# A scheduler advance of 300 instructions for reads of the accumulator in a two-layer hybrid block

## The chip, the cores and the metric

The kernel runs on one core of a Trainium2 chip. The metric is the device time of one execution in microseconds (us), all of it fp32 work. Engines are named as in the profile: PE is TensorE, DVE is VectorE, ACT is ScalarE, POOL is GpSimd, SP is the engine that issues most transfers; PEld is PE's loading of the stationary operand.

## The reference, cut to what matters

Two layers over 640 tokens (128 context, 512 latent), each a token mixer and a feed-forward block, with 1024 channels:

```python
m = jax.nn.silu(cond) @ p['w_ada'] + p['b_ada']            # six modulation vectors
h = rms_norm(x, p['norm1']) * (1 + sc1) + sh1
q, k, v, og, gkf, gkb, sb, sc, sx, fx, mg = jnp.split(h @ p['w_in'], pts, axis=-1)
o = gla_bidir(q, k, v, la_f, la_b, s0_f, s0_b)             # 4 heads, chunks of 64, both directions
y_a = (norm(o) * silu(og)) @ p['w_a_out']
y_b = (sb * dwconv3(sc * sx, conv_w)) @ p['w_b_out']
y_c = real(fft2(fx)) @ p['w_c_out']
x = x + g1 * ((g[0] * y_a + g[1] * y_b + g[2] * y_c) @ p['w_o'])   # g: sigmoid of mg
h = rms_norm(x, p['norm2']) * (1 + sc2) + sh2
x = x + g2 * ((silu(gate) * up) @ w_down)                  # gate, up = split(h @ w_up)
```

The change lies in how `h @ w_in` (and, in a few places, `h @ w_up`) leaves the accumulator, and in the reads of the gated linear attention (GLA) heads that run between.

## The kernel before

**Products.** Tokens lie along the free axis (640, in halves of 320), channels on the partitions. Every product keeps fp32 accuracy by three matmuls: high part by high part, high by low, low by high. Weights are streamed by SP into buffers `raw` (six of 1024 columns); the high part `whi` is a cast on ACT (line 139), the low part `wlo` a subtraction on DVE (line 140), each into three buffers of 1024 columns. PE takes them in the order of the stream, and the split runs two chunks ahead. In mean a matmul of 128x128 by 128x320 follows the one before it by the distance that the rows below show.

**Pairs.** Most of `w_in` and `w_up` goes through `pair` (line 249): two column blocks together, with seven half-size products of 12 matmuls where eight would be plain. The accumulator space (PSUM) is handed out as four tiles of two banks. A pair N of the mixer has the tile `w1p_Nb` for its bank y and `w1p_Na` for its banks x and b. In program order a pair does: product into x; ACT copies x to `s1` (line 276); product T1 into b; ACT copies b to `s5` (line 280); product T2 into y; DVE adds y to `s1` (line 283); ACT writes `s1` back into y (line 284); DVE adds `s1` to b (line 285); then 24 matmuls into x and b (B21 and B22), after which `done` copies the first result block out (for instance line 966); then product T3 into y; DVE adds `s5` to y for half of the second block (line 296); and, put off into the next pair by `last`, product T4 into y and the copy of y (line 300). So the 24 matmuls into `w1p_Na` wait for line 285, and T3 into `w1p_Nb` waits for line 284. Weight sums that the pair needs (`sb`, `sc`, lines 160 to 167) are made on DVE. There are 24 pairs in each mixer and 19 in each feed-forward block.

**Between products.** `tick_bg` steps generators that put other work between the products: a GLA head (`gla_head`: gate products `lg` at line 639, read by ACT at lines 641 and 642; two scans on DVE at lines 646 and 647; state steps on DVE at line 696, 14 in a head; attention products `af` and `ab` at line 703, read by DVE at lines 704 and 705; output products read by ACT at lines 719 and 720), and pieces of the modulation of the next layer (`ada`: products at line 371, ACT copy at line 377, transposes at line 380, DVE reduction at line 383). They take their PSUM tiles from the same four.

**What sets the order.** The order of instructions on each engine is made ahead of time by a list scheduler: among the instructions whose inputs its model takes for ready, the one with the lowest priority number goes first, and that number is the place in the program as written. Each engine then runs its list strictly in that order. Nothing in the code sets another priority.

Of the kernel before, what the change touches and what calls it, by code (L numbers as in the profile page):

```python
# [14 lines left out]
AF = mybir.ActivationFunctionType  # L15
ALU = mybir.AluOpType
# [7 lines left out]
T = 640  # L24
TH = 320
# [66 lines left out]
class Builder:  # L92
    def __init__(self, stack, tc, a):
        self.tc = tc
        self.nc = tc.nc
        self.a = a
        self.cp = stack.enter_context(tc.tile_pool(name="cp", bufs=1))
        self.wp = stack.enter_context(tc.tile_pool(name="wp", bufs=1))
        self.up = stack.enter_context(tc.tile_pool(name="up", bufs=N_UNITS))
        self.pp = stack.enter_context(tc.tile_pool(name="pp", bufs=4, space=PSUM))  # L100
        self.dp = stack.enter_context(tc.tile_pool(name="dp", bufs=1, space=DRAM))
        self.n = 0
        self.gens, self.later, self.ada_last, self.last_act, self.pending = [], [], None, None, None
# [144 lines left out]
    def pair(self, key, h, T12, T34, done):  # L248

        nc = self.nc

        def prod(o, w, c0, ops, first):
            for kb in range(4):
                sl = slice(c0 + kb * P, c0 + kb * P + P)
                lh, ll = w[0][:, sl], w[1][:, sl]  # L260
# [12 lines left out]
        x, b = p1[:, 0:TH], p1[:, 512:512 + TH]
        prod(x, wa, 0, B11, True)
        s1 = self.wp.tile([P, TH], F32, tag="s1", name=self.name("s1"), bufs=1)
        nc.scalar.copy(s1, x)
# [12 lines left out]
        prod(x, wa, 512, B21, False)  # L289
        del wa  # L290
        w = self.take(key, "c")
        prod(b, w, 0, B22, False)
        done(0, pv(p1))
        prod(y, w, 512, T3, False)
        z = self.wp.tile([P, T], F32, tag="z", name=self.name("z"), bufs=3)
        nc.vector.tensor_add(z[:, TH:T], y, s5)

        def last():
            prod(y, d, 0, T4, False)
            nc.scalar.copy(z[:, 0:TH], y)  # L300
# [72 lines left out]
    def ada_end(self, l, v, n, ps):  # L373
        nc = self.nc
        p = self.par[l]
        u = self.unit(cols=256, s="adas")
        nc.scalar.copy(u, ps[:, 0:256])
# [5 lines left out]
        nc.vector.tensor_reduce(mv, pm.rearrange("p (k j i) -> p k i j", k=2, i=32)[:, :, 0:2, :], op=ALU.add, axis=mybir.AxisListType.X)  # L383
# [250 lines left out]
    def gla_head(self, l, hd, gk, qd, kd, v, yos):  # L634
        nc = self.nc
        p = self.par[l]
        ps = self.psum("lg")
        for h in range(2):
            nc.tensor.matmul(ps[:, h * 512:h * 512 + TH], p["w_gk"][:, hd, :], gk[:, h * TH:h * TH + TH], start=True, stop=True)
        u1, u2, bc = self.unit(s="u1"), self.unit(s="u2"), self.unit(s="bc")  # L640
        nc.scalar.activation(halves(u1), pv(ps), AF.Abs, bias=p["b_gk"][:, hd:hd + 1])
        nc.scalar.activation(halves(u2), pv(ps), AF.Relu, bias=p["nb_gk"][:, hd:hd + 1], scale=-1.0)
# [17 lines left out]
        g = self.cp.tile([P, NCHUNK], F32, tag="g", name=self.name("g"), bufs=2)  # L660
# [6 lines left out]
        yield  # L667
        pt = self.to_tokens(ko)
        koT = self.unit(s="koT")
        nc.scalar.copy(koT, pt[:, 0:T])  # L670
# [14 lines left out]
        for half, d0, s0, n, r in ((0, 1, 0, 2, 0), (0, 6, 3, 1, 0), (0, 9, 2, 1, 0), (0, 2, 0, 2, 1), (0, 5, 2, 2, 1),  # L685
                                   (1, 1, 1, 1, 0), (1, 4, 3, 2, 0), (1, 0, 0, 2, 1), (1, 3, 2, 2, 1), (1, 8, 4, 1, 1)):
            hs = slice(64 * half, 64 * half + 64)
            nc.scalar.copy(sv[hs, d0:d0 + 2 * n - 1:2], uv[r][hs, s0:s0 + n])
        fin = self.cp.tile([P, P], F32, tag="fin", name=self.name("fin"), bufs=1)
        nc.vector.scalar_tensor_tensor(fin[0:64], sv[0:64, 9], g[0:64, 9:10], uv[1][0:64, 4], ALU.mult, ALU.add)  # L690
        nc.vector.scalar_tensor_tensor(fin[64:128], sv[64:128, 8], g[64:128, 4:5], uv[0][64:128, 2], ALU.mult, ALU.add)
# [12 lines left out]
        nc.vector.copy_predicated(self.zf, self.mask[:, 0], af[:, 0:T])  # L704
        nc.vector.copy_predicated(self.zb, self.mask[:, 1], ab[:, 0:T])
        am = self.unit(s="am")
        nc.vector.tensor_add(am, self.zf, self.zb)
        yield
# [10 lines left out]
        nc.scalar.activation(sq, po[:, 0:T], AF.Square)  # L719
        nc.scalar.activation(yo, po[:, 0:T], AF.Copy, scale=p["gla_norm"])  # L720
        yield
        pn = self.psum("on")
        for h in range(2):
# [199 lines left out]
    def mixer(self, l, h, hx, hps):  # L923
# [9 lines left out]
        def v_out(t):  # L933
            pt = self.to_tokens(t)
            u = self.unit(s="v")
            nc.scalar.copy(u, pt[:, 0:T])
            v.append(u)

        def split(t):
# [22 lines left out]
        def sbuf(z, o):  # L962
            if z:
                return o
            t = self.wp.tile([P, T], F32, tag="z", name=self.name("z"), bufs=3)
            nc.scalar.copy(halves(t), o)
            return halves(t)

        def out(nm, z, o):
            c = nm[z]  # L970
            if c >= MG0:
                nc.sync.dma_start(halves(self.sgd[c - MG0]), sbuf(z, o))
            elif c >= FX0:
                f, o = self.fxd[c - FX0], sbuf(z, o)
                nc.sync.dma_start(f[:, 0:NLAT].rearrange("p (h t) -> p h t", h=2), lat(o))
                nc.sync.dma_start(f[:, NLAT:T].rearrange("p (h t) -> p h t", h=2), ctx_(o))
            elif c >= SX0:
                cb[c - SX0] = self.conv(l, c - SX0, cb[c - SX0], o)
            elif c >= SC0:
                cb[c - SC0] = sbuf(z, o)  # L980
            elif c >= SB0:
                t = cb.pop(c - SB0)
                nc.vector.tensor_mul(halves(t), o, halves(t))
                bb[c - SB0] = split(t)
            elif c >= OG0:
# [224 lines left out]
```

## Time and profile before

| | us |
|---|---|
| median of 3 runs (lowest to highest) | 2141.34 (2139.84 to 2142.73) |
| the profiled execution | 2140.18 |
| span of its trace | 2138.3 |
| PE busy | 2049.9 |
| PEld busy | 1940.5 |
| DVE busy | 1459.8 |
| ACT busy | 1041.2 |
| POOL busy | 18.2 |

The span leaves 1.9 us of the profiled execution outside the trace, and the profiled execution lies 1.16 us below the median. Busy times of PE are of pipelined matmuls: a matmul's own duration is about twice its distance from the next, so a sum of durations says nothing, and idle time of PE is read from the wait rows.

### The profile page before, as it was taken

Reading aid. Unit: us, or ns where it says so; the run is one execution under the profiler, and the core shown is the slowest. Engines: PE = TensorE matmul, PEld = TensorE weight load, DVE = VectorE, ACT = ScalarE, POOL = GpSimd, SP = SyncE. Lnnn points to the kernel's source line nnn. Section 1 sums busy time; section 2 is a strip of 40 time slices with the busy share of each in tenths; the row PEclk is TensorE's granted clock in tenths of the full one; section 3 lists DMA queues with packets and bytes.
Section 4 is the critical chain, followed back from the end, with each engine's and each line's share of the span. In section 5 each row is a group of like instructions: output and inputs, shape, how many; then the busy total and the mean of one; then the engine's idle time right before and its main releaser. Section 6 shows DMA issues by size and latency. Waiting matters only on the chain.

```text
span 2138.3 us, 35359 instructions
## 1 busy us (share of the span) xinstructions
PE 2049.9 (96%) x14100; PEld 1940.5 (91%) x14100; DVE 1459.8 (68%) x2422; ACT 1041.2 (49%) x1743; POOL 18.2 (1%) x52
## 2 busy tenths in 40 slices
PE   5999999999999999999999999999999999999997
PEld 2898988999998999999978888889999999999997
DVE  5676778666667676666576776787575776666766
ACT  5555555555454334344466555555543643343443
POOL 2000000000000000000000000000000000000000
PEclk9999999999999999999999999999999999999999
DMA  8244433554512333332332534335554122222222
GB/s 319 67 148 155 148 121 116 172 188 141 198 47 65 109 102 97 107 117 87 102 109 96 169 137 135 111 118 174 188 170 143 55 62 82 70 86 69 79 74 70
DMA packets 99973, 256.74 MB, mean 120 GB/s; under 512 B 13344, under 2 KB 31968, under 8 KB 99808
## 3 DMA queue, kind: packets, MB, share of 16 engines
q1 hardware_dynamic: 95360, 250.91, 35.2%
q10 hardware_dynamic: 3728, 2.49, 0.4%
q8 instruction: 111, 1.82, 0.3%
q0 software_dynamic: 720, 1.07, 0.1%
q14 instruction: 54, 0.44, 0.1%
HBM read 227.69 MB, written 26.74 MB: 119 GB/s over the span
## 4 chain that ended last, share of the span: by engine, by line
PE 84%; DVE 8%; ACT 4%; issue 1%; DMA 1%; ACTq 0%; DVEq 0%
PE wd L245 14%; PE wb L245 8%; PE wo L245 3%; PE w L245 2%; PE ada L371 2%; PE wu L245 2%; DVE S L696 1%; ACT whi L139 1%; DVE wlo L140 1%; PE o L717 1%; PE w1p_50a L263 1%; PE w1p_12a L263 1%; PE w1p_18a L263 1%; PE w1p_42a L263 1%; PE w1p_46a L263 1%
## 5 line engine op out<-in xcount | busy, mean ns | idle before, releaser
L139 ACT CAST whi<-raw 128x512 fp32r<-128x512 f32 (+2 forms) x368 | 270.2, 735 | 354.1 <-PE wd L245 50.4
L140 DVE TENSOR_TENSOR wlo<-raw,whi 128x512 fp32r<-128x512 f32 (+2 forms) x368 | 303.7, 829 | 148.8 <-ACT whi L139 144.4
L245 PE MATMUL wd<-ffhi,whi 128*128 128x320 f32 x656 | 154.6, 315 | 12.6 <-ACT whi L139 12.6
L245 PE MATMUL wd<-fflo,whi 128*128 128x320 f32 x656 | 149.9, 309 | 0.0
L245 PE MATMUL wd<-ffhi,wlo 128*128 128x320 f32 x656 | 149.5, 309 | 0.0
L502 DVE SCALAR_TENSOR_TENSOR x<-wd,mod,x 128x512 f32<-128x512 f32 x212 | 108.7, 545 | 54.5 <-PE wd L245 54.3
L140 DVE TENSOR_TENSOR wlo<-sb,whi 128x1024 fp32r<-128x1024 f32 x86 | 105.0, 1221 | 57.7 <-ACT whi L139 56.7
L245 PEld LDWEIGHTS wd<-ffhi,whi 128*128 128x128 f32 x656 | 108.9, 188 | 23.7 <-ACT whi L139 20.4
L139 ACT CAST whi<-sc 128x1024 fp32r<-128x1024 f32 x86 | 90.0, 1047 | 56.1 <-PE wd L245 27.6
L139 ACT CAST whi<-sb 128x1024 fp32r<-128x1024 f32 x86 | 90.1, 1048 | 52.8 <-PE wd L245 11.6
L140 DVE TENSOR_TENSOR wlo<-sc,whi 128x1024 fp32r<-128x1024 f32 x86 | 104.7, 1218 | 8.0 <-ACT whi L139 7.8
L245 PEld LDWEIGHTS wd<-fflo,whi 128*128 128x128 f32 x656 | 109.7, 188 | 0.0
L245 PEld LDWEIGHTS wd<-ffhi,wlo 128*128 128x128 f32 x656 | 109.7, 188 | 0.0
L160 DVE TENSOR_TENSOR sb<-raw 128x512 f32<-128x512 f32 x86 | 59.1, 687 | 29.9 <-DMA raw<-in_w 29.2
L371 PE MATMUL ada<-raw,cond 128*32 128x256 f32 x768 | 57.3, 402 | 13.4 <-ACT cond L410 5.8
L166 DVE TENSOR_TENSOR sc<-raw,sb 128x512 f32<-128x512 f32 x86 | 59.5, 691 | 2.6
L161 DVE TENSOR_TENSOR sb<-sb,raw 128x512 f32<-128x512 f32 x86 | 59.1, 687 | 0.8
L245 PE MATMUL wb<-bhi,whi 128*128 128x320 f32 x256 | 59.2, 312 | 0.0
L167 DVE TENSOR_TENSOR sc<-raw,raw 128x512 f32<-128x512 f32 x86 | 58.9, 684 | 0.0
L245 PE MATMUL wb<-blo,whi 128*128 128x320 f32 x256 | 58.3, 309 | 0.0
L245 PE MATMUL wb<-bhi,wlo 128*128 128x320 f32 x256 | 58.3, 309 | 0.0
L330 ACT CAST ffhi<-ff 128x640 fp32r<-128x640 f32 x44 | 32.0, 727 | 45.7 <-DVE ff L1078 45.5
(1264 smaller groups left out, 6213.5 us busy)
## 6 DMA issues: line engine op xcount, KB each, us to landing
raw<-in_w SPq DMA_DIRECT2D x104, 512.0 KB, 4.3
raw<-in_w_ada SPq DMA_DIRECT2D x96, 512.0 KB, 4.4
raw<-in_wu SPq DMA_DIRECT2D x88, 512.0 KB, 3.5
raw<-in_wd SPq DMA_DIRECT2D x96, 192.0 KB, 2.4
sgd<-z SPq DMA_DIRECT2D x48, 320.0 KB, 4.2
sgl<-sgd SPq DMA_DIRECT2D x48, 320.0 KB, 3.5
raw<-in_wb SPq DMA_DIRECT2D x48, 256.0 KB, 2.7
raw<-in_wo SPq DMA_DIRECT2D x16, 512.0 KB, 3.5
```

Source lines behind the costliest of these rows:

```text
L139: self.nc.scalar.copy(hi[:, 0:n], src)
L140: self.nc.vector.tensor_sub(lo[:, 0:n], src, hi[:, 0:n].bitcast(F32))
L160: nc.vector.tensor_add(sb[:, 0:512], a21, a22)
L161: nc.vector.tensor_sub(sb[:, 512:1024], sb[:, 0:512], a11)
L166: nc.vector.tensor_sub(sc[:, 0:512], a12, sb[:, 512:1024])
L167: nc.vector.tensor_sub(sc[:, 512:1024], a11, a21)
L245: nc.tensor.matmul(o[h], w[:, sl], rhs[kb][h][part], start=(kb == 0 and first), stop=(kb == nk - 1 and last))
L263: nc.tensor.matmul(o, l, r, start=(first and kb == 0 and n == 0), stop=(kb == 3 and n == 2), skip_group_check=not first)
L330: self.nc.scalar.copy(hi, src)
L371: self.nc.tensor.matmul(ps[32 * j:32 * j + 32, 0:256], self.cond[:, 4 * kp + j, :], r[:, j, :], start=(kp == 0), stop=(kp == 1))
L502: self.nc.vector.scalar_tensor_tensor(seg(xv), seg(v), g[:, j, i:i + 1], seg(xv), ALU.mult, ALU.add)
L696: nc.vector.scalar_tensor_tensor(sv[hs, i + d], sv[hs, i], g[hs, LAT[i]:LAT[i] + 1], sv[hs, i + d], ALU.mult, ALU.add)
```

## The change

A constant `SOON = 300` and a method `soon()` that gives the scheduler's `high_priority(offset=300)`: what stands inside it gets a number 300 lower, as if it stood 300 instructions earlier in the program. `soon()` is put around the instructions that read or rewrite the accumulator, one by one. No instruction, tile, buffer or transfer is added or removed: PE, ACT, DVE, SP and POOL have the same instructions in another order.

```diff
+SOON = 300
...
+    def soon(self):
+        return self.tc.high_priority(offset=SOON)
...
-        nc.scalar.copy(s1, x)
+        with self.soon():
+            nc.scalar.copy(s1, x)
...
-        nc.scalar.copy(s5, b)
+        with self.soon():
+            nc.scalar.copy(s5, b)
...
-        nc.vector.tensor_add(s1, y, s1)
-        nc.scalar.copy(y, s1)
-        nc.vector.tensor_add(b, b, s1)
+        with self.soon():
+            nc.vector.tensor_add(s1, y, s1)
+        with self.soon():
+            nc.scalar.copy(y, s1)
+        with self.soon():
+            nc.vector.tensor_add(b, b, s1)
...
-        nc.vector.tensor_add(z[:, TH:T], y, s5)
+        with self.soon():
+            nc.vector.tensor_add(z[:, TH:T], y, s5)
...
-            nc.scalar.copy(z[:, 0:TH], y)
+            with self.soon():
+                nc.scalar.copy(z[:, 0:TH], y)
```

The same is put around the copies and reductions of the modulation pieces (lines 377 and 383), the two gate reads (641 and 642), the copy of the transposed keys (670), the copies of `u` into `S` and the two final states (688, 690, 691), the two masked copies (704, 705), the two reads of the head's output (719, 720), and the copies of finished blocks out of the accumulator (936, 966, 989).

Order, place 1: ACT in pair 4 of layer 0, from the copy of x on. `qk` are the copies of earlier q and k blocks, the table load belongs to an activation function that comes next, `whi_111` is the high part of a weight chunk. Before:

```order
L276 COPY s1_110_801<-w1p_0_4a_109_788 128x320
L330 CAST thi_98_714<-t34_95_705 128x640
L931 ACTIVATE qk_100_718<-w1_0_2_75_613 128x640
L931 ACTIVATE qk_105_776<-w1_0_3_104_727 128x640
L406 ACT_TABLE_LOAD
L139 CAST whi_111_803<-raw_21_0_421 128x1024
L280 COPY s5_113_819<-w1p_0_4a_109_788 128x320
L284 COPY w1p_0_4b_114_821<-s1_110_801 128x320
L139 CAST whi_118_858<-sb_117_855 128x1024
```

and now:

```order
L282 COPY s1_110_801<-w1p_0_4a_109_788 128x320
L342 CAST thi_98_714<-t34_95_705 128x640
L955 ACTIVATE qk_100_718<-w1_0_2_75_613 128x640
L287 COPY s5_113_819<-w1p_0_4a_109_788 128x320
L955 ACTIVATE qk_105_776<-w1_0_3_104_727 128x640
L420 ACT_TABLE_LOAD
L293 COPY w1p_0_4b_114_821<-s1_110_801 128x320
L144 CAST whi_111_803<-raw_21_0_421 128x1024
L144 CAST whi_118_858<-sb_117_855 128x1024
```

The copy to `s5` moves ahead of the second `qk`, and the write-back into y moves ahead of the cast `whi_111`; both stood behind the table load and the cast. On DVE the addition into b (line 285) moves ahead of the low part that stood before it, and on PE the 24 matmuls into `w1p_4a` move ahead of the seven of T3 that they followed. In layer 1 the 24 stood first, and one of T3 now stands ahead of them.

Order, place 2: DVE ahead of pair 46 of layer 0, where the attention products `af` of a head are read. `S` are the state steps, `wlo` low parts of weights. Before:

```order
L696 SCALAR_TENSOR_TENSOR S_340_2428<-S_340_2428,g_308_2194 64x128 x7
L140 TENSOR_TENSOR wlo_346_2491<-sb_344_2487,whi_345_2490 128x1024
L696 SCALAR_TENSOR_TENSOR S_340_2428<-S_340_2428,g_308_2194 64x128
L296 TENSOR_TENSOR z_348_2521<-w1p_0_44b_337_2394,s5_336_2392 128x320
L704 COPY_PREDICATED zf_185_1341<-mask_84,af_349_2523 128x640
L140 TENSOR_TENSOR wlo_355_2556<-sc_353_2552,whi_354_2555 128x1024
L705 COPY_PREDICATED zb_186_1342<-mask_84,ab_350_2524 128x640
```

and now:

```order
L716 SCALAR_TENSOR_TENSOR S_340_2428<-S_340_2428,g_308_2194 64x128 x5
L145 TENSOR_TENSOR wlo_346_2491<-sb_344_2487,whi_345_2490 128x1024
L716 SCALAR_TENSOR_TENSOR S_340_2428<-S_340_2428,g_308_2194 64x128
L307 TENSOR_TENSOR z_348_2521<-w1p_0_44b_337_2394,s5_336_2392 128x320
L716 SCALAR_TENSOR_TENSOR S_340_2428<-S_340_2428,g_308_2194 64x128
L145 TENSOR_TENSOR wlo_355_2556<-sc_353_2552,whi_354_2555 128x1024
L725 COPY_PREDICATED zf_185_1341<-mask_84,af_349_2523 128x640
L727 COPY_PREDICATED zb_186_1342<-mask_84,ab_350_2524 128x640
L716 SCALAR_TENSOR_TENSOR S_340_2428<-S_340_2428,g_308_2194 64x128
```

Of the state steps one moves behind the masked copy `zf`, and the low part `wlo_355` moves ahead of it.

Order, place 3: DVE in pair 48 of layer 0, around the two scans of a head (`bc`). Before:

```order
L645 TENSOR_TENSOR u2_379_2721<-u2_379_2721,u1_378_2720 128x640
L646 SCALAR_TENSOR_TENSOR bc_380_2722<-scanm_184_1340,u2_379_2721 64x640
L647 SCALAR_TENSOR_TENSOR bc_380_2722<-scanm_184_1340,u2_379_2721 64x640
L283 TENSOR_TENSOR s1_386_2765<-w1p_0_48b_390_2785,s1_386_2765 128x320
L140 TENSOR_TENSOR wlo_392_2816<-raw_48_1_2550,whi_391_2815 128x512
L140 TENSOR_TENSOR wlo_388_2768<-raw_49_0_2559,whi_387_2767 128x1024
L285 TENSOR_TENSOR w1p_0_48a_385_2752<-w1p_0_48a_385_2752,s1_386_2765 128x320
L383 TENSOR_REDUCE mod0_107<-ada_381_2730 128x4
```

and now:

```order
L661 TENSOR_TENSOR u2_379_2721<-u2_379_2721,u1_378_2720 128x640
L662 SCALAR_TENSOR_TENSOR bc_380_2722<-scanm_184_1340,u2_379_2721 64x640
L291 TENSOR_TENSOR s1_386_2765<-w1p_0_48b_390_2785,s1_386_2765 128x320
L663 SCALAR_TENSOR_TENSOR bc_380_2722<-scanm_184_1340,u2_379_2721 64x640
L295 TENSOR_TENSOR w1p_0_48a_385_2752<-w1p_0_48a_385_2752,s1_386_2765 128x320
L397 TENSOR_REDUCE mod0_107<-ada_381_2730 128x4
L145 TENSOR_TENSOR wlo_388_2768<-raw_49_0_2559,whi_387_2767 128x1024
L145 TENSOR_TENSOR wlo_392_2816<-raw_48_1_2550,whi_391_2815 128x512
```

The addition into `s1` (now line 291) moves between the two scans, and the addition into b (now line 295) and the reduction move ahead of two low parts. On ACT the write-back into y keeps its place behind the cast `whi_387`, and on PE the 24 matmuls into `w1p_48a` now follow the first five of T3, where all twelve stood ahead of them.

Elsewhere the moves are of the same kind: instructions of ACT move by at most six places, of DVE by at most fifteen. In the feed-forward blocks ACT's order is unchanged, and the moves lie in ten pairs of layer 0. On SP eight transfers of finished blocks move ahead of a weight load.

## Rows read from the trace of the kernel before

**Rows 1.** The page: span; busy time, share and instructions of each engine; the chain of work that ended last, by engine.
```profile
span 2138.3 us, 35359 instructions
...
PE 2049.9 (96%) x14100; PEld 1940.5 (91%) x14100; DVE 1459.8 (68%) x2422; ACT 1041.2 (49%) x1743; POOL 18.2 (1%) x52
...
PE 84%; DVE 8%; ACT 4%; issue 1%; DMA 1%; ACTq 0%; DVEq 0%
```

**Rows 2.** Waits of PE over the whole span: the waiting tile and line, what it waited for, then us in total, times, longest.
```profile
PE w1p_48b L263 <- ACT w1p_48b L284: 4.6, 2, 2.3
...
PE w1p_17b L263 <- DVE z L296: 2.9, 2, 1.5
PE w1p_32a L263 <- DVE w1p_32a L285: 2.9, 2, 1.6
PE w1p_4b L263 <- ACT w1p_4b L284: 2.9, 1, 2.9
PE w1p_8a L263 <- DVE wlo L140: 2.5, 2, 1.2
...
PE w1p_4a L263 <- DVE w1p_4a L285: 1.5, 1, 1.5
...
PE w1p_40b L263 <- ACT w1p_40b L284: 1.1, 2, 0.7
PE w1p_10a L263 <- ACT z L966: 1.0, 2, 0.5
...
PE w1p_46a L263 <- DVE zf L704: 1.0, 2, 0.5
...
PE w1p_24b L263 <- DVE zf L704: 0.4, 2, 0.2
PE w1p_38b L263 <- DVE zf L704: 0.4, 2, 0.2
```

**Rows 3.** Timeline of pair 4 in layer 0: start, duration, engine, line, operation, tiles; in brackets the idle time before and what ended it.
```profile
79.18 1.29 ACT L931 ACTIVATE qk<-w 128x640 f32<-128x640 f32 x2
...
80.49 1.28 ACT L406 ACT_TABLE_LOAD   x1
81.05 0.49 DVE L283 TENSOR_TENSOR s<-w1p_4b,s 128x320 f32<-128x320 f32 x1
81.78 1.04 ACT L139 CAST whi<-raw 128x1024 fp32r<-128x1024 f32 x1
82.73 0.42 ACT L280 COPY s<-w1p_4a 128x320 f32<-128x320 f32 x1
...
83.05 0.43 ACT L284 COPY w1p_4b<-s 128x320 f32<-128x320 f32 x1
...
83.54 0.41 PE L263 MATMUL w1p_4b<-thi,whi 128*128 128x320 f32 x1 [2.87 <-ACT w1p_4b L284]
...
83.79 0.31 PE L263 MATMUL w1p_4b<-tlo,whi 128*128 128x320 f32 x1
...
84.52 0.31 PE L263 MATMUL w1p_4b<-thi,whi 128*128 128x320 f32 x1
```

**Rows 4.** Timeline of pair 4 in layer 1, same columns.
```profile
1130.47 1.31 ACT L931 ACTIVATE qk<-w 128x640 f32<-128x640 f32 x2
...
1131.34 0.50 DVE L285 TENSOR_TENSOR w1p_4a<-w1p_4a,s 128x320 f32<-128x320 f32 x1
...
1131.89 0.56 PE L263 MATMUL w1p_4a<-hhl,whi 128*128 128x320 f32 x2 [1.49 <-DVE w1p_4a L285]
```

**Rows 5.** Timeline ahead of pair 46 in layer 0.
```profile
247.33 0.35 DVE L696 SCALAR_TENSOR_TENSOR S<-S,g 64x128 f32<-64x128 f32 x1
247.72 0.49 DVE L296 TENSOR_TENSOR z<-w1p_44b,s 128x320 f32<-128x320 f32 x1
248.13 0.86 DVE L704 COPY_PREDICATED zf<-mask,af 128x640 f32<-128x640 uint8 x1
...
248.88 1.21 DVE L140 TENSOR_TENSOR wlo<-sc,whi 128x1024 fp32r<-128x1024 f32 x1
249.04 0.56 PE L263 MATMUL w1p_46a<-hhl,whi 128*128 128x320 f32 x2 [0.50 <-DVE zf L704]
```

**Rows 6.** Timeline of pair 48 in layer 0, to the first matmul of the next pair.
```profile
274.98 1.48 DVE L646 TENSOR_TENSOR_SCAN bc<-scanm,u 64x640 f32<-64x640 f32 x1
...
276.23 1.04 ACT L139 CAST whi<-raw 128x1024 fp32r<-128x1024 f32 x1 [0.16 <-PE w1p_48b L263]
276.47 1.49 DVE L647 TENSOR_TENSOR_SCAN bc<-scanm,u 64x640 f32<-64x640 f32 x1
277.99 0.49 DVE L283 TENSOR_TENSOR s<-w1p_48b,s 128x320 f32<-128x320 f32 x1
...
278.52 0.43 ACT L284 COPY w1p_48b<-s 128x320 f32<-128x320 f32 x1 [1.25 <-DVE s L283]
...
279.00 0.41 PE L263 MATMUL w1p_48b<-thi,whi 128*128 128x320 f32 x1 [2.30 <-ACT w1p_48b L284]
...
280.13 0.49 DVE L285 TENSOR_TENSOR w1p_48a<-w1p_48a,s 128x320 f32<-128x320 f32 x1
...
285.92 0.31 PE L263 MATMUL w1p_16a<-hhl,whi 128*128 128x320 f32 x1
```

**Rows 7.** Stretch around pair 48 of layer 0: from and to, length, then busy time and instructions of PE, PEld, DVE, ACT, POOL; PE's granted clock as a share of full, DMA share, GB/s.
```profile
270.00:285.00 15.00, 12.49 (x73) 11.98 (x73) 9.21 (x14) 9.24 (x16) 0.00 (x0) 0.89 0.44 158
```

More of the change, by code (lines that the diff above doesn't have):

```diff
@@ L376, in ada_end @@
         u = self.unit(cols=256, s="adas")
-        nc.scalar.copy(u, ps[:, 0:256])
+        with self.soon():
+            nc.scalar.copy(u, ps[:, 0:256])
         pm = ps[:, 512:768]
@@ L382, in ada_end @@
         mv = p["mod"][:, v, ks]
-        nc.vector.tensor_reduce(mv, pm.rearrange("p (k j i) -> p k i j", k=2, i=32)[:, :, 0:2, :], op=ALU.add, axis=mybir.AxisListType.X)
+        with self.soon():
+            nc.vector.tensor_reduce(mv, pm.rearrange("p (k j i) -> p k i j", k=2, i=32)[:, :, 0:2, :], op=ALU.add, axis=mybir.AxisListType.X)
         nc.vector.tensor_add(mv, mv, p["b_ada"][:, v, ks])
@@ L640, in gla_head @@
         u1, u2, bc = self.unit(s="u1"), self.unit(s="u2"), self.unit(s="bc")
-        nc.scalar.activation(halves(u1), pv(ps), AF.Abs, bias=p["b_gk"][:, hd:hd + 1])
-        nc.scalar.activation(halves(u2), pv(ps), AF.Relu, bias=p["nb_gk"][:, hd:hd + 1], scale=-1.0)
+        with self.soon():
+            nc.scalar.activation(halves(u1), pv(ps), AF.Abs, bias=p["b_gk"][:, hd:hd + 1])
+        with self.soon():
+            nc.scalar.activation(halves(u2), pv(ps), AF.Relu, bias=p["nb_gk"][:, hd:hd + 1], scale=-1.0)
         self.act(u1, u1, AF.Exp, scale=-1.0)
@@ L669, in gla_head @@
         koT = self.unit(s="koT")
-        nc.scalar.copy(koT, pt[:, 0:T])
+        with self.soon():
+            nc.scalar.copy(koT, pt[:, 0:T])
         yield
@@ L687, in gla_head @@
             hs = slice(64 * half, 64 * half + 64)
-            nc.scalar.copy(sv[hs, d0:d0 + 2 * n - 1:2], uv[r][hs, s0:s0 + n])
+            with self.soon():
+                nc.scalar.copy(sv[hs, d0:d0 + 2 * n - 1:2], uv[r][hs, s0:s0 + n])
         fin = self.cp.tile([P, P], F32, tag="fin", name=self.name("fin"), bufs=1)
-        nc.vector.scalar_tensor_tensor(fin[0:64], sv[0:64, 9], g[0:64, 9:10], uv[1][0:64, 4], ALU.mult, ALU.add)
-        nc.vector.scalar_tensor_tensor(fin[64:128], sv[64:128, 8], g[64:128, 4:5], uv[0][64:128, 2], ALU.mult, ALU.add)
+        with self.soon():
+            nc.vector.scalar_tensor_tensor(fin[0:64], sv[0:64, 9], g[0:64, 9:10], uv[1][0:64, 4], ALU.mult, ALU.add)
+        with self.soon():
+            nc.vector.scalar_tensor_tensor(fin[64:128], sv[64:128, 8], g[64:128, 4:5], uv[0][64:128, 2], ALU.mult, ALU.add)
         nc.scalar.dma_start(self.a["out_state"][l, :, hd, :], fin)
@@ L703, in gla_head @@
                 nc.tensor.matmul(o[:, sl], kin[64 * half:64 * half + 64, sl], qin[64 * half:64 * half + 64, sl], start=True, stop=True)
-        nc.vector.copy_predicated(self.zf, self.mask[:, 0], af[:, 0:T])
-        nc.vector.copy_predicated(self.zb, self.mask[:, 1], ab[:, 0:T])
+        with self.soon():
+            nc.vector.copy_predicated(self.zf, self.mask[:, 0], af[:, 0:T])
+        with self.soon():
+            nc.vector.copy_predicated(self.zb, self.mask[:, 1], ab[:, 0:T])
         am = self.unit(s="am")
@@ L718, in gla_head @@
         sq, yo = self.unit(s="osq"), self.unit(s="yo")
-        nc.scalar.activation(sq, po[:, 0:T], AF.Square)
-        nc.scalar.activation(yo, po[:, 0:T], AF.Copy, scale=p["gla_norm"])
+        with self.soon():
+            nc.scalar.activation(sq, po[:, 0:T], AF.Square)
+        with self.soon():
+            nc.scalar.activation(yo, po[:, 0:T], AF.Copy, scale=p["gla_norm"])
         yield
@@ L935, in v_out @@
             u = self.unit(s="v")
-            nc.scalar.copy(u, pt[:, 0:T])
+            with self.soon():
+                nc.scalar.copy(u, pt[:, 0:T])
             v.append(u)
@@ L965, in sbuf @@
             t = self.wp.tile([P, T], F32, tag="z", name=self.name("z"), bufs=3)
-            nc.scalar.copy(halves(t), o)
+            with self.soon():
+                nc.scalar.copy(halves(t), o)
             return halves(t)
@@ L988, in out @@
                 t = self.unit(s="vf")
-                nc.scalar.copy(halves(t), o)
+                with self.soon():
+                    nc.scalar.copy(halves(t), o)
                 self.later.append(lambda: v_out(t))
```

## The prediction

> **What bounds the kernel now.** I read the page first: PE is busy for 2049.9 of 2138.3 us, and 84% of the chain that ended last is PE, with 8% on DVE and 4% on ACT [rows 1]. So a read of the accumulator is worth something only where PE stands still for it. Next come PE's waits. Those that this change can touch are the named ones on lines 284, 285, 296, 704 and 966 and the wait for a low part at pair 8 [rows 2]. Together they are 4.6 + 2.9 + 2.9 + 2.9 + 2.5 + 1.5 + 1.1 + 1.0 + 1.0 + 0.4 + 0.4 = 21.2 us, about 1% of the time, over both layers. That is the pot, to which only the clock adds something (below). Third, the timeline around the largest of them shows what each late read stood behind, and the order of the changed kernel shows whether that thing is still ahead of it.
>
> PE's pace is the unit. In pair 4 the matmuls from 83.79 to 84.52 are five steps, so one step is 0.73 / 5 = 0.146 us [rows 3].
>
> **The change part by part.** The set of instructions is the same, so no duration is added; every term is a shift.
>
> Pair 4, layer 0. T3 waits 2.87 us, until 83.54, for the write-back at 83.05, which stood behind a table load (1.28), a cast (1.04) and the copy to s5 (0.42) on ACT [rows 3]. In the new order the copy to s5 comes behind the first of two qk copies (1.29 for both), the addition into b follows the addition into s1 at once, and PE takes the 24 matmuls first. They need the addition into b, not the write-back: 81.05 + 0.49 = 81.54, plus another 0.50 for the addition [rows 3, 4] and 0.05 to reach PE (in layer 1 the addition ends at 1131.84 and PE starts at 1131.89 [rows 4]), so about 82.1. Gain 83.54 - 82.1 = 1.4 us. The cast that loses its place comes about 1.1 us later; it hides behind the 24 + 12 matmuls that now run (36 x 0.146 = 5.3 us). A gain is excluded from being over 2.9, the whole wait.
>
> Pair 4, layer 1. The 24 started at 1131.89, straight after the addition into b [rows 4]. Now one matmul of T3 stands ahead of them and needs the write-back, which needs ACT to be through both qk copies (1130.47 + 1.31 = 1131.78 [rows 4]) and then 0.43 for itself [rows 3], so 1132.2, and one step for the matmul: 1132.4. Loss 0.5 us.
>
> Pair 46, both layers. PE waits for the masked copy zf, which begins at 248.13 [rows 5]. One state step of 0.35 us moves behind it and a low part of 1.21 us moves ahead of it, on an engine without a pause there: loss 1.21 - 0.35 = 0.86 us a layer.
>
> Pair 48, both layers. The addition into s1 stood behind both scans (until 277.96) and ran at 277.99; the write-back followed at 278.52, and PE began T3 at 279.00 after 2.30 us [rows 6]. Now the addition stands between the scans. On ACT the cast of 1.04 us stays ahead of the write-back and waits for PE, so it bounds the write-back from below at 276.23 + 1.04 = 277.27. The first gate reads move one copy earlier, which brings scans and products forward by 0.2 to 0.5 us. I place the write-back at 277.3 to 277.7, five matmuls of T3 from 277.75 (ending about 278.5), the second scan to about 278.7, the addition into b to 279.2, the 24 from 279.25, the other seven of T3 to 279.25 + 31 x 0.146 = 283.8. Before, the next pair began at 285.92 [rows 6]. That is 2.1 us earlier, if PE keeps its full clock.
>
> The clock is 1.6 of these 2.1. The granted clock is 0.89 over 270 to 285 us [rows 7], and the 36 matmuls from 279.00 to 285.92 took 6.92 us where 36 x 0.146 = 5.26 [rows 6, 3]: 1.66 us lost to a drop from 2.4 to 1.2 GHz behind the 2.30-us wait. The wait of 2.87 us at pair 4 was followed by no drop, as its steps of 0.146 us show [rows 3]. So a wait alone does not decide it. In the new order the standstill is cut in two, about 1.5 and 0.75 us, with five matmuls between. I take it that the clock then stays; the other value (it drops all the same) is a rival. Gain 0.5 + 1.6 a layer.
>
> Small ones, both layers: pair 38 waits 0.2 for zf behind two state steps that move away, pair 24 the same [rows 2], and both then start up to 0.3 us earlier with the start of a copy; +0.3 each. Pair 10: the copy at line 966 moves ahead of a cast, and the wait of 0.5 goes: +0.5. Pair 17: the wait of 1.5 for line 296 goes, since that addition passes nine state steps of 0.35 us [rows 2, 5], but T4 then runs after the first products of pair 18, whose addition into b closes the same unbroken run of DVE work; DVE's work up to that addition falls by one step, so +0.3 and not +1.5. Pair 8: its wait of 1.2 for a low part goes, but the additions of pair 8 stay behind the exponentials and the three products with the keys of a head, which start no earlier; +0.1. Pair 40: its additions get between the scans (1.48 each [rows 6]), while one more copy stands behind the gate reads; 0, with ends of -0.3 and +0.7. Pair 32 waits 1.6 a layer [rows 2] in an order that is unchanged: 0. The moves in ten feed-forward pairs of layer 0 touch places where PE has no named wait on these lines: 0, and -0.1 to +0.1 each. On SP eight transfers of results go ahead of a weight load; with six raw buffers and no wait of a pair for a load in the rows: 0. At the start, where modulation pieces move ahead of splits, PE stands still for other things: +0.2, with ends of -0.3 and +0.7.
>
> Sum for layer 0: 1.4 - 0.86 + 0.5 + 0.3 + 0.3 + 0.5 + 0.3 + 0.1 = 2.5; for layer 1 with -0.5 in place of 1.4: 0.6; start 0.2. That is 3.3 us, and 2 x 1.6 = 3.2 for the clock: 6.5 us. The profiled execution (2138.3 in the span and 1.9 outside it, 2140.2 us) becomes 2133.7; the median stands 1.16 above it: 2134.8 us.
>
> **The rivals.**
>
> (a) The clock drops at pair 48 all the same, since nearly as much idle time is left there (2.2 of 2.3 us). For it: both layers dropped at the same place, so it is not chance. Against it: pair 4 stood still for longer and did not. Then only 3.3 us come: 2141.3 - 3.3 = 2138.0. The Trainium skill (TensorE: Matmul & The Clock Gate, A second HAM failure mode: psum-queue depth-cycling) tells of a kernel in which short idle times between groups of matmuls, from cycling through accumulator banks, took the clock up and down between its two levels. By that rule two short standstills in place of one would not save the clock, which is this rival's time; the trace agrees at pair 48 (0.89) and disagrees at pair 4, so it stays the second case and not the first.
>
> (b) DVE's order is the bound. The waits on lines 284 and 296 have DVE work behind them, and the chain already has 8% of DVE [rows 1]; if the moved additions still end behind scans and state steps, each wait comes back one product later, as I expect at pair 17. Then the gains of pairs 17, 48, 38, 24 and 8 go and the clock drops: 1.4 - 0.5 - 1.7 + 1.0 + 0.2 leaves +0.4, 2141 us.
>
> (c) Slower: reads put forward hold up the splits. A read that stands earlier in an engine's list and whose product is still running keeps casts and low parts behind it waiting, and PE's weights come late. Row for it: pair 8 already waits 1.2 for a low part [rows 2], so there a split has no slack. The price is one copy, 0.43 us [rows 3], for each pair whose split is late; it decides as soon as more than 8 pairs in the two mixers (8 x 0.43 = 3.4) are so hit, and with 20 of the 48 the sum is 3.3 - 8.6 = -5.3 us: 2146.6. Against it: DVE is busy for 68% and ACT for 49% [rows 1], the split runs two chunks ahead, and the low part is named for one pair only. The Trainium skill (PSUM — Partial Sum Buffer, Engine vs sequencer instructions) says that the queues of ScalarE and VectorE are strictly first in, first out, which is what this rival needs; the table load and cast ahead of the s5 copy in pair 4 agree with it [rows 3].
>
> (d) Much faster: all the touchable waits go, 21.2 less the 2.9 of pair 32 whose order is the same, plus 3.2 for the clock: 21.5 us, 2119.8. It needs every read to be on time, against the scans.
>
> **How the numbers follow.** Forecast with the clock kept 0.45, (a) 0.27, (b) 0.15, (c) 0.09, (d) 0.04. The likeliest gives 2134.8, 0.3% faster. Its own uncertainty is some 3 us (the ends named above, and a term like pair 46 that I read wrongly in either layer). The range takes in (a) and (b) and leaves out (d) and most of (c): 2129 to 2143. About 0.2% (4.3 us) is what a measurement of this kernel can tell from no change, so faster means under 2137.1. Faster: 0.45 x 0.83 + 0.27 x 0.37 + 0.04, about 0.52. Slower: most of (c) and a little of (b), 0.09. Same: 0.39.
>
> **What would show it.** In the profile after: the wait of `w1p_4b` for line 284 (2.87) gone and one of `w1p_4a` for line 285 of about 1.4 in its place; in layer 1 a wait there of about 2.0 in place of 1.5; `w1p_46a` waiting for zf 1.3 in place of 0.5; at pair 48 two waits in place of one, and a granted clock near 1.00 from 270 to 285 and 1320 to 1335 us; no 1.5 at `w1p_17b`, but a like wait at `w1p_18a`; pair 32 as before. The prediction is wrong if low parts (line 140) turn up as what pairs wait for, or if pair 48 keeps 0.89.

## The result

The median fell from 2141.34 us (2139.84 to 2149.12, 5 runs) to 2131.28 us (2130.8 to 2133.1, 5 runs): 10.1 us, a ratio of 0.9948 with a 95% interval of 0.993 to 0.9966. The forecast was 2134.8 us with a range of 2129 to 2143, so the time lies inside, on the fast side. The sum that led there was not right in its parts, as the waits and the clock show.

The page of the changed kernel, the lines that answer to [rows 1]:

```profile
span 2129.5 us, 35360 instructions
...
PE 2049.1 (96%) x14100; PEld 1939.9 (91%) x14100; DVE 1460.2 (69%) x2422; ACT 1043.4 (49%) x1743; POOL 18.3 (1%) x52
...
PE 85%; DVE 8%; ACT 4%; issue 1%; DMA 1%; ACTq 0%; DVEq 0%
```

The span less PE's busy time is the first thing to read: 2138.3 - 2049.9 = 88.4 us before, 2129.5 - 2049.1 = 80.4 after. Of the 8.8 us between the two spans 8.0 are less standing still, and only 0.8 are busy time. Time at a lower clock counts as busy, so the clock made no more than 0.8 us between these two executions; the mean granted clock of both is 0.994.

One execution of each is not the whole record, though. The granted clock of every run is known: 0.9933 in the mean of the 42 runs of the kernel before that stand beside the experiments, 0.9948 in that of 10 runs of the changed kernel. What is missing to 1, times the span, is 14.3 and 11.1 us. So some 3 us of the difference between the medians can be clock. That is an estimate from above, since PE does not set the pace everywhere; within the runs of one kernel (116 runs of all kernels) the time falls by about 1.4 us for each 0.001 of clock, which would make it 2 us.

In the changed kernel the lines of the pair are 282, 287, 291, 293, 295, 307 and 312 (before 276, 280, 283, 284, 285, 296 and 300), those of the splits 144 and 145, of the scans 662 and 663, of the masked copies 725 and 727.

PE's waits in the changed kernel, the answer to [rows 2] (tile and line, what was waited for, us in total, times, longest):

```profile
PE w1p_32a L268 <- DVE w1p_32a L295: 2.5, 2, 1.3
...
PE w1p_46a L268 <- DVE zf L725: 2.5, 2, 1.2
...
PE w1p_48b L268 <- ACT w1p_48b L293: 2.1, 2, 1.1
...
PE w1p_18a L268 <- DVE w1p_18a L295: 1.8, 2, 0.9
PE w1p_4b L268 <- ACT w1p_4b L293: 1.8, 1, 1.8
PE w1p_8b L268 <- ACT w1p_8b L293: 1.6, 2, 0.8
PE w1p_4a L268 <- DVE w1p_4a L295: 1.5, 1, 1.5
PE w1p_40a L268 <- DVE w1p_40a L295: 1.4, 2, 0.7
...
PE w1p_48a L268 <- DVE w1p_48a L295: 1.2, 2, 0.6
...
PE w1p_19a L268 <- ACT s L282: 1.1, 2, 0.5
```

The reader should see three things. In pair 4 of layer 0 a wait of 2.9 for the write-back has become one of 1.5 for the addition into b, and in pair 48 one of 4.6 for the write-back has become 2.1 for it and 1.2 for the addition. The wait of 2.9 in pair 17 has become one of 1.8 in pair 18. And pair 46 is worse, 2.5 in place of 1.0. Pair 4 of layer 0, pair 4 of layer 1, and the low part and the masked copy ahead of pair 46:

```profile
84.42 0.41 PE L268 MATMUL w1p_4a<-hhl,whi 128*128 128x320 f32 x1 [1.52 <-DVE w1p_4a L295]
...
1127.03 0.41 PE L268 MATMUL w1p_4b<-thi,whi 128*128 128x320 f32 x1 [1.76 <-ACT w1p_4b L293]
...
247.28 1.23 DVE L145 TENSOR_TENSOR wlo<-sc,whi 128x1024 fp32r<-128x1024 f32 x1
248.42 0.86 DVE L725 COPY_PREDICATED zf<-mask,af 128x640 f32<-128x640 uint8 x1
```

The timeline of pair 48, from its first matmul to the first of the next pair, beside [rows 6]:

```profile
268.99 0.56 PE L268 MATMUL w1p_48a<-hhl,whi 128*128 128x320 f32 x2
...
275.41 1.48 DVE L662 TENSOR_TENSOR_SCAN bc<-scanm,u 64x640 f32<-64x640 f32 x1
275.66 1.05 ACT L144 CAST whi<-raw 128x1024 fp32r<-128x1024 f32 x1 [0.56 <-PE w1p_48b L268]
276.82 0.46 DVE L291 TENSOR_TENSOR s<-w1p_48b,s 128x320 f32<-128x320 f32 x1
277.30 1.49 DVE L663 TENSOR_TENSOR_SCAN bc<-scanm,u 64x640 f32<-64x640 f32 x1
277.31 0.43 ACT L293 COPY w1p_48b<-s 128x320 f32<-128x320 f32 x1 [0.60 <-DVE s L291]
277.79 0.41 PE L268 MATMUL w1p_48b<-thi,whi 128*128 128x320 f32 x1 [1.07 <-ACT w1p_48b L293]
...
279.38 0.56 PE L268 MATMUL w1p_48a<-hhl,whi 128*128 128x320 f32 x2 [0.59 <-DVE w1p_48a L295]
...
284.02 0.46 PE L268 MATMUL w1p_16a<-hhl,whi 128*128 128x320 f32 x2
```

The addition (276.82) lies between the scans and the standstill is cut in two, 1.07 and 0.59 us. The clock, by stretch (PE's granted clock is the third number from the end):

```profile
270.00:285.00 15.00, 13.34 (x88) 12.63 (x88) 10.49 (x17) 10.94 (x19) 0.00 (x0) 1.00 0.41 153
36.00:48.00 12.00, 11.76 (x75) 6.36 (x76) 6.38 (x22) 8.79 (x18) 0.00 (x0) 0.73 0.80 278
1120.00:1135.00 15.00, 12.31 (x70) 11.32 (x69) 10.94 (x17) 8.91 (x13) 2.07 (x5) 0.89 0.11 37
1700.00:1720.00 20.00, 17.36 (x103) 16.07 (x102) 15.16 (x28) 8.01 (x14) 0.00 (x0) 0.91 0.04 11
```

Pair 48 has its full clock, as forecast, in both layers. But there are drops at pair 4 of layer 1 (0.89) and at the first feed-forward pair of layer 1 (tile `wup_3`; the expectations call it the third; 0.91), where the kernel before kept 1.00 (1120 to 1140 and 1700 to 1720 us), and a longer one at the start.

### The profile page after: what moved, and what is told of

Same layout as the page of the kernel before. It is cut to its first block, busy times and chain, and to the rows that moved or that the text cites. A ratio compares the mean times of both kernels' runs of the same rounds, so it can differ in the third digit from the quotient of the medians.

```text
span 2129.5 us, 35360 instructions
## 1 busy us (share of the span) xinstructions
PE 2049.1 (96%) x14100; PEld 1939.9 (91%) x14100; DVE 1460.2 (69%) x2422; ACT 1043.4 (49%) x1743; POOL 18.3 (1%) x52
## 3 DMA queue, kind: packets, MB, share of 16 engines
q0 software_dynamic: 720, 1.07, 0.1%
## 4 chain that ended last, share of the span: by engine, by line
PE 85%; DVE 8%; ACT 4%; issue 1%; DMA 1%; ACTq 0%; DVEq 0%
PE wd L250 14%; PE wb L250 8%; PE wo L250 3%; PE ada L383 2%; PE wu L250 1%; DVE wlo L145 1%; ACT whi L144 1%; PE w L250 1%; PE o L739 1%; PE u L699 1%; PE w1p_50a L268 1%; PE w1p_36a L268 1%; PE w1p_46a L268 1%; PE w1p_10a L268 1%; PE w1p_24a L268 1%
```

## The experiments

Of each kernel with a time, the waits of PE at four places are summed over both layers, from its wait rows (us); the span less the busy time follows, then the median and the ratio to the kernel before on the same chip. The four sums repeat when a program runs again; "not busy" moves by about 2 us (changed, no S copies). It is no clean measure of the waits that the order makes, nor busy time of the clock: "no modulation", with a mean granted clock of 0.997, has 5.5 us more standing still than the changed kernel with 0.994, as much less busy time, and the same span.

| kernel | 48 and 16 | 17 and 18 | 46 | 19 and 8 | not busy | median, ratio (interval) |
|---|---|---|---|---|---|---|
| before | 5.0 | 3.4 | 1.0 | 2.8 | 88.4 | 2141.3 |
| changed | 3.3 | 1.8 | 2.5 | 2.7 | 80.4 | 2131.3, 0.9948 (0.993 to 0.9966) |
| pairs only | 3.9 | 3.4 | 1.2 | 3.9 | 86.2 | 2140.0, 0.999 (0.998 to 1.0001) |
| rest only | 4.2 | 2.1 | 2.5 | 3.2 | 86.0 | 2136.9, 0.9976 (0.9967 to 0.9986) |
| pairs, gates | 3.3 | 3.4 | 1.2 | 2.6 | 85.8 | 2133.2, 0.9954 (0.994 to 0.9967) |
| pairs, gates, masked copies | 3.3 | 1.8 | 1.2 | 2.6 | 79.5 | 2132.1, 0.9948 (0.9935 to 0.9962) |
| no modulation | 3.3 | 1.9 | 2.5 | 2.7 | 85.9 | 2130.9, 0.9949 (0.993 to 0.9968) |
| no S copies | 3.3 | 1.7 | 1.2 | 2.7 | 80.1 | 2133.0, 0.9956 (0.9939 to 0.9974) |
| no modulation, no S | 3.3 | 1.7 | 1.2 | 2.7 | 81.5 | 2130.8, 0.9947 (0.9932 to 0.9962) |
| no line 296 | 3.3 | 2.1 | 2.5 | 5.5 | 84.4 | 2134.7, 0.996 (0.9945 to 0.9975) |
| before, shifted | 5.0 | 3.4 | 1.0 | 2.8 | 91.2 | 2145.8, 1.0015 (1.0006 to 1.0025) |
| changed, shifted | 3.3 | 1.8 | 2.5 | 2.7 | 81.7 | 2133.7, 0.9961 (0.9946 to 0.9976) |
| changed, once more | 3.3 | 1.8 | 2.5 | 2.7 | 82.2 | 2130.8, 0.9944 (0.993 to 0.9957) |
| no S copies, once more | 3.3 | 1.7 | 1.2 | 2.7 | 82.4 | 2130.8, 0.9941 (0.9929 to 0.9954) |

**Pairs only.** My first theory was that the pairs' own reads make the gain.

```diff
         with self.soon():
             nc.scalar.copy(s1, x)
...
-        with self.soon():
-            nc.scalar.copy(u, ps[:, 0:256])
+        nc.scalar.copy(u, ps[:, 0:256])
```

(and so for every read outside `pair`)

> The advance stays on the seven reads of the pairs alone. Theory A (the gain is made by the pairs' own additions and copies passing splits, scans and state steps, the other advances cost or do nothing): pair 4 of layer 0, pair 48 and pair 17/18 gain as in the changed kernel, pair 46 and the start lose nothing, total 2129 to 2133 us. Theory B (the gate reads and masked copies of the heads make the gain, by starting the scans earlier): under 3 us of gain, 2138 to 2141 us, and pair 48 keeps its wait of about 2.3 us.

```profile
PE w1p_8b L268 <- ACT w1p_8b L293: 3.2, 2, 1.7
PE w1p_18a L268 <- DVE zf L716: 2.9, 2, 1.4
PE w1p_48b L268 <- ACT w1p_48b L293: 2.6, 2, 1.3
...
PE w1p_16a L268 <- ACT z L312: 1.3, 2, 0.7
```

2140.0 us: the gain is all but gone, and theory A falls. B's time came (2138 to 2141), but not its sign: the wait at pair 48 fell from 2.3 to 1.3 a layer. Pair 4 gained as forecast, but at pair 17/18 the wait only changed its name (the masked copy zf at 18 in place of line 296 at 17), and pair 48 passed part of its wait on to pair 16.

**The rest only.** The same, the other way round: every read in `pair` without the advance.

> The advance stays on all reads but those of the pairs. Theory A: the loss ahead of pair 4 (2.2 us) and at pair 46 (0.76 a layer) remain, the gains at pairs 10 and 38 (0.5 and 0.3 a layer) remain, total 2141 to 2144 us. Theory B: 2133 to 2137 us.

```profile
PE w1p_16a L268 <- DVE wlo L145: 3.1, 2, 1.6
...
PE w1p_8a L268 <- DVE wlo L145: 2.5, 2, 1.2
PE w1p_46a L268 <- DVE zf L718: 2.5, 2, 1.2
PE w1p_18a L268 <- DVE w1p_18a L290: 2.1, 2, 1.1
...
PE w1p_16a L268 <- ACT z L305: 1.1, 2, 0.5
```

2136.9 us, at the upper end of B's forecast and well under A's. But B does not carry the change either: alone the two parts gain 1.3 and 4.4 us, together 10. Pair 48's wait moved to pair 16 here too, onto a low part. So a third theory, C: the gain arises where an advanced read of a pair meets an advanced read of a head. The waits in the table do not ask for it by themselves: at pairs 48 and 16 the two parts take off 1.1 and 0.8 alone and 1.7 together, at 17 and 18 nothing and 1.3 alone and 1.6 together, which nearly adds up. And part of the excess in time is clock: the two halves have a mean granted clock of 0.9937 and 0.9939, near the 0.9935 of the kernel before beside them, the changed kernel 0.9946 and 0.9950 in its two sets of runs.

**Pairs and gates, then the masked copies too.** Lines 641 and 642 with the pairs, then 704 and 705 as well.

> The advance on the pairs' reads and on the two gate reads of the heads (lines 641 and 642 before), nowhere else. Theory C (the two sets need each other at pair 48: the gate reads bring the scans forward, the pair's addition then fits between them): PE's waits in pair 48 and at the start of pair 16 sum to about 1.7 us a layer, as in the changed kernel, where the pairs alone or the rest alone gave 2.1; pairs 17 and 18 keep 1.7 (their gain comes from the masked copies); total 2136 to 2139 us. Rival: the gate reads make no difference to the pairs-alone kernel, 2.1 stays, total 2140.

> As the kernel before this one in the list, with the two masked copies (lines 704 and 705 before) advanced too. If they make the gain at pairs 17 and 18, the waits there fall from 1.7 to about 1.0 us a layer, those of pairs 24 and 38 vanish (0.3 each), pair 46 stays at 0.6 because the copies into S are not advanced; total 2131 to 2134 us. If these three sets do not carry the gain, 2136 or more.

Pairs and gates:

```profile
PE w1p_18a L268 <- DVE zf L718: 2.9, 2, 1.4
...
PE w1p_48b L268 <- ACT w1p_48b L293: 2.1, 2, 1.1
...
PE w1p_48a L268 <- DVE w1p_48a L295: 1.2, 2, 0.6
```

With the masked copies:

```profile
PE w1p_48b L268 <- ACT w1p_48b L293: 2.1, 2, 1.1
PE w1p_18a L268 <- DVE w1p_18a L295: 1.8, 2, 0.9
```

Both waits moved where C put them: pair 48 and 16 from 3.9 to 3.3 with the gate reads, pairs 17 and 18 from 3.4 to 1.8 with the masked copies. C's reason at pair 48 does not hold, though: the scans did not come forward. The first one begins 6.3 us after the pair's first matmul in the kernel before (268.70 and 274.98) and 6.4 in the changed one (268.99 and 275.41), as in this kernel; only DVE's order changed, with the addition now between the two scans. The gate reads without the pairs' were not run, so that the two sets need each other is not shown. In time the first came out better than expected (2133.2 against 2136 to 2139), though its not-busy time of 85.8 us is nearly that of the pairs alone: of the 6.8 us between their spans (2139.6 and 2132.8) 6.4 are PE's busy time (2053.4 and 2047.0), where the clock is counted. The three sets together came to 2132.1 us, 10.9 of the 12.2 us by which the changed kernel beat the one before beside them.

**No S copies; no modulation reads; neither.** The advance taken from lines 688, 690 and 691, from 377 and 383, and from both.

> The changed kernel without the advance on the copies of u into S and on the two final states. PE's order is the same to the instruction. If they are what puts a low part ahead of the masked copy at pair 46, PE waits there 0.4 to 0.6 us as before the change (1.2 with it), 0.76 us a layer, total about 2129.8 us. Rival: the masked copy's own advance makes that loss, then 1.2 us stay and the total is unchanged at 2131.3.

> The changed kernel without the advance on the two reads of the modulation pieces. If these make the 2.2 us that the changed kernel loses before pair 4 starts, pair 4 begins near 75.2 us instead of 77.5, and the total is about 2129 us. If that loss is only where PE's granted clock happens to fall, pair 4 still begins after 76.5 us and the total stays near 2131.

> The changed kernel without the advance on the modulation reads and on the copies into S and the final states together. By the sums of waits: pair 46 back to 0.6 us a layer, the modulation advance worth nothing in time; total 2129.5 to 2131.5 us, the fastest so far. If the two are tied up with each other (or with the clock), 2132 to 2135.

```profile
PE w1p_46a L268 <- DVE zf L722: 1.2, 2, 0.6
```

Without the advance on the S copies pair 46 waits 1.2 us in place of 2.5, with PE's order the same to the instruction: they put the low part ahead of the masked copy, not that copy's own advance. The times do not follow: 2133.0, 2130.9 and 2130.8 us, all within the spread of the changed kernel. The modulation reads are no cause of the late start: without their advance pair 4 began at 77.2 us, with it at 77.5, before at 75.2; and the kernel without the S advance, whose order up to there is that of the changed one, began it at 75.8 in one execution and at 78.5 in another.

**No line 296.**

```diff
-        with self.soon():
-            nc.vector.tensor_add(z[:, TH:T], y, s5)
+        nc.vector.tensor_add(z[:, TH:T], y, s5)
```

> The changed kernel without the advance on the addition of s5 (line 296 before). If that advance makes the gain at pairs 17 and 18, PE waits there 1.7 us a layer again in place of 1.0, and the total is about 1.5 us longer, 2132.8 us. If the earlier scans make it, the wait stays near 1.0 and the total at 2131.3.

```profile
PE w1p_8a L268 <- DVE w1p_8a L295: 4.4, 2, 2.5
...
PE w1p_18a L268 <- DVE w1p_18a L295: 2.1, 2, 1.1
```

The wait at pair 17/18 hardly rose, so my step there is refuted; pair 8 lost instead (4.4 us there on the addition into b, where the changed kernel waited 1.6 for the write-back), and the median is 3.5 us above that of the changed kernel; by the ratios, whose intervals overlap, it is 2.6 to 3.4. This one advance pays two pairs later than where I looked.

**A shift in time.** Two extra additions of 0.82 us on DVE at the start, all else in the same order, for the kernel before and the changed one:

```diff
             nc.vector.tensor_add(self.sq_acc, self.sq_acc, s)
+            if j == 7:
+                nc.vector.tensor_add(self.sq_acc, self.sq_acc, s)
+                nc.vector.tensor_sub(self.sq_acc, self.sq_acc, s)
```

> The kernel before with two extra additions of 0.82 us on DVE, in a row, before the first norm's sum goes to PE (the last summand is added and taken away again, so the sum changes by rounding only). The order of all else is the same to the instruction, so everything behind 24 us comes about 1.9 us later. If the waits of PE decide where its granted clock falls, the drops stay at pair 48 of both layers and at the third feed-forward pair of layer 0, and the total is 2141.3 + 1.9 = 2143.2 us. If the moment at which a wait comes decides, other waits are followed by drops, and the total lies off 2143.2 by one or more drops of about 1.7 us.

> The changed kernel with the same two extra additions. If waits decide: drops as in the changed kernel (long one at the start, at pair 4 and the third feed-forward pair of layer 1, none at pair 48), total 2131.3 + 1.9 = 2133.2 us. If the moment decides: drops elsewhere, total off 2133.2 by one or more times 1.7 us.

The kernel before, shifted: its wait row, the first matmul of pair 48 and of the next pair in layer 0, then its stretches. The last line of the first block is the first matmul of pair 48 without the shift:

```profile
PE w1p_48b L263 <- ACT w1p_48b L284: 4.6, 2, 2.3
...
273.02 0.56 PE L263 MATMUL w1p_48a<-hhl,whi 128*128 128x320 f32 x2
...
288.70 0.46 PE L263 MATMUL w1p_16a<-hhl,whi 128*128 128x320 f32 x2
...
268.70 0.56 PE L263 MATMUL w1p_48a<-hhl,whi 128*128 128x320 f32 x2
```

```profile
270.00:290.00 20.00, 17.50 (x119) 15.53 (x118) 14.54 (x22) 15.01 (x25) 0.00 (x0) 1.00 0.43 134
200.00:220.00 20.00, 17.91 (x116) 15.20 (x115) 14.14 (x21) 13.59 (x22) 0.00 (x0) 0.91 0.43 151
1320.00:1340.00 20.00, 17.49 (x111) 15.74 (x110) 13.65 (x20) 13.87 (x23) 0.00 (x0) 0.91 0.38 123
```

The wait at pair 48 is the same to 0.1 us. In layer 0 it is followed by no drop now (1.00; 0.89 in [rows 7]), in layer 1 still by one, and around pair 40 (200 to 220 us, 1.00 unshifted) there is a new one, as there is at 1120 to 1140 and at 1360 to 1380 us (0.91 each, 1.00 unshifted). The median is 2145.8 us, ratio 1.0015 (1.0006 to 1.0025): 3.2 us for 1.9 us of shift against the 2142.6 beside it. The changed kernel, shifted, took 2133.7 us (2131.4 to 2138.6), ratio 0.9961 (0.9946 to 0.9976), close to the 2133.2 expected if the waits decide. Its drops speak for both sides:

```profile
660.00:680.00 20.00, 17.32 (x102) 16.11 (x101) 12.14 (x23) 9.00 (x16) 0.00 (x0) 0.91 0.17 43
...
1120.00:1140.00 20.00, 17.31 (x103) 16.08 (x102) 13.98 (x20) 10.99 (x16) 2.07 (x5) 0.91 0.09 28
```

Those at pair 4 and at `wup_3` of layer 1 stayed (0.91 and 0.91), pair 48 kept 1.00 in both layers, the long one at the start is gone (1.00 from 36 to 48 us), and one at 660 to 680 us is new (1.00 unshifted).

**Once more.** The changed kernel and the one without the S advance, side by side.

> The changed kernel once more, unchanged. If the program alone fixes where the granted clock falls, its drops stand where they stood (long one at the start, pair 4 and the third feed-forward pair of layer 1) and the waits of the pairs repeat; median within 1 us of 2131.3. If the moment of a run decides, the waits repeat to 0.05 us and the drops do not.

> The changed kernel without the advance on the copies into S and the final states, timed beside the unchanged one. By PE's waits it is 1.2 us better (0.62 a layer at pair 46); by the clock, anything within 2 us. Median 2129.5 to 2132 us; waits of the pairs as in its first run.

The changed kernel, one stretch, then the kernel without the S advance around pair 48 of layer 0, first and second time:

```profile
1700.00:1720.00 20.00, 17.24 (x113) 16.18 (x112) 16.08 (x29) 8.89 (x15) 0.00 (x0) 1.00 0.04 11
```

```profile
270.00:290.00 20.00, 18.35 (x111) 17.60 (x111) 16.20 (x25) 11.68 (x20) 0.00 (x0) 0.91 0.26 97
270.00:290.00 20.00, 18.34 (x121) 17.39 (x120) 15.45 (x24) 13.52 (x23) 0.00 (x0) 1.00 0.40 138
```

The same program has the same waits in its pairs (table). In the changed kernel the drop at 1700 to 1720 us (0.91) is gone, that at pair 4 of layer 1 is there again (0.89). Without the S advance, with PE's order the same to the instruction, the clock dropped at pair 48 the first time and not the second, and at pair 4 of layer 1 likewise. Medians: 2130.8 us for the changed kernel (ratio 0.9944, 0.993 to 0.9957), 2130.8 without the S advance (0.9941, 0.9929 to 0.9954). So the version that has 1.3 us less waiting cannot be told from the changed one by its time. Its 10 runs have a mean granted clock of 0.9939 and the changed kernel's 10 have 0.9948, which is some 2 us of span the other way; that can hide the gain, and whether it does is open.

## Why the prediction was right, and where it was not

- **Pair 4, layer 0:** forecast a gain of 1.4. PE waited 2.87 us before and 1.52 after, and the kernel without the pairs' advance waits 2.9. The step is right.
- **Pair 4, layer 1:** forecast a loss of 0.5. The wait came where it was expected, for the write-back; the waits of the two tiles went from 2.4 to 2.7 us, so 0.3 was lost. The drop that followed there (0.89) cost more, and was not foreseen.
- **Pair 46:** forecast a loss of 0.86 a layer; it was (2.5 - 1.0) / 2 = 0.75. The mechanism is as read from the order; its cause is the advance on the S copies.
- **Pair 48, the whole:** forecast 2.1 a layer, with T3 at 277.75, the 24 at 279.25 and the next pair at 283.8; found 277.79, 279.38 and 284.02, in a pair that began 0.3 us later. From the first matmul of the pair to the first of the next it took 17.2 us (268.70 to 285.92) and now takes 15.0 (268.99 to 284.02): 2.2, the same in layer 1. The shifted kernel before, which waited as long and kept its clock, took 15.7 (273.02 to 288.70). So of the 2.2 some 1.5 are the clock and 0.7 the wait, against 1.6 and 0.5 in the forecast; the wait rows give (5.0 - 3.3) / 2 = 0.85 for the wait. One step in it was wrong: the gate reads did not bring the scans forward by 0.2 to 0.5 us.
- **Pair 48, the reason for the clock:** that cutting the standstill in two keeps the clock is not shown. The single wait kept its clock once, in layer 0 of the shifted kernel before, so of its four stretches in two traces three had a drop. With the standstill cut, in ten traces, three stretches of twenty had one (no S copies, and pairs with gates and masked copies, in layer 0; no modulation in layer 1). That speaks for fewer drops, not for none, and two traces of the kernel before are few.
- **The clock elsewhere:** forecast no change, without a reason. This is the term that failed. What the two traces save at pair 48 they spend at the start, at pair 4 and at `wup_3` of layer 1: PE's busy time, which holds the time at the lower clock, fell by 0.8 us and not 3.2. Over all runs 2 to 3 us of clock may have been gained after all, near the 3.2 forecast, but that does not bear out the reason given for it.
- **Pairs 17 and 18:** forecast 0.3 a layer; it was (3.4 - 1.8) / 2 = 0.8, mainly from the masked copies (3.4 to 1.8 when they were added) and not from line 296 (2.1 without its advance, 1.8 with it). This is the stall term most undersized.
- **Pair 10:** forecast 0.5 and it came, but not by the advance on line 966: with the pairs alone the wait is gone, with the rest alone, line 966 among it, 0.5 a layer stays.
- **Pairs 24 and 38:** 0.2 each where 0.3 was forecast; **pair 8 with 19:** no more than 0.1 a layer, as forecast; **pair 40:** 0 was forecast and some 0.3 a layer came. It came from two waits that the pot of 21.2 us had left out, though their reads were advanced: on the gate read of line 642 (1.0 us in all before, 0.7 after) and on the copy of line 300 (1.7 and 1.2).
- **Pair 34:** forecast nothing, its order is the same. It waited 1.2 us in all before, 0.3 after, 0.7 in the second run of the same program, and 2.0 in the shifted kernel before. What moves it is open.
- **The start:** forecast 0.2; pair 4 began 2.2 us later, with the clock at 0.73 from 36 to 48 us. The same order up to there gave 75.8 and 78.5 us in two executions of the kernel without the S advance, so the start differs by more than 2 us from one execution to the next, and the late one is no work of the order. The granted clock has a part in it (36 to 48 us: 0.91 in the early one, 0.72 in the late one), but the kernel without the modulation reads began at 77.2 with 0.86.

So the total came inside the range in part by luck. The median fell by 10.1 us where 6.5 was forecast. Between the two traces 8.0 us of standing still and under 1 us of clock were found, where 3.3 and 3.2 were forecast: the waits were summed too low, at pairs 17, 18 and 40 above all, and the clock's gain at pair 48 was lost again at places that the sum had left out. Of the rivals, (a) has the net of the clock between the two traces but not its place: the drop at pair 48 did go. (b) describes what the pairs' advances do alone (0.4 us forecast for it, 1.3 measured). (c) did not appear: no pair of the changed kernel waits for the low part of a weight (`wlo`) any more, pair 8 included. At pair 46 a low part moved ahead of a read, the other way round from (c), and cost 0.75 us a layer, as forecast; a new wait for a low part did appear with the rest alone, at pair 16 (3.1 us).

## What to carry to other kernels

What an advance in a scheduler's order is worth shows only when the wait that it removes has been followed to the next consumer: with one set of reads alone, part of pair 48's wait turned up at pair 16 and the wait of pair 17 at pair 18. So cost a reordering by following each wait to what is late next, and try sets of reads rather than single ones. And where a kernel's clock drops after short waits, sum the change of PE's waits apart from the clock, take the clock from all runs and not from one trace, and do not forecast a gain from one drop that disappears while leaving the other places out of the sum.

## What was not expected of the hardware

Whether the granted clock fell behind a wait was not settled by the wait. The same wait of 2.3 us at pair 48 was followed by 0.89 in one execution and by 1.00 in the kernel shifted by 1.9 us; the same program kept or lost the clock at 1700 to 1720 us (0.91 and 1.00) in two executions, and another program, the one without the S advance, at pair 48 (0.91 and 1.00). Yet the drops are not spread at random: that at pair 4 of layer 1 came in all three traces of the changed kernel, the shifted one among them. One drop cost 1.5 us at pair 48 (17.2 against 15.7 us), so it alone moves this kernel's time by 0.07%, and the runs of one kernel spread over more than that (2136.7 to 2146.1 us for the kernel before on one chip). The Trainium skill (TensorE: Matmul & The Clock Gate, A second HAM failure mode: psum-queue depth-cycling) tells of a clock that goes up and down between its two levels over short idle times between groups of matmuls; the trace agrees that it does, and shows beyond it that the same idle time may or may not be followed by a drop.
